# q and k written as high and low parts, and the output norm's root in fused VectorE steps

## The chip, the cores and the metric

One Trainium2 chip, of which the program uses one core. The metric is the device time of one execution of the program in microseconds (us): the median of several runs. One further execution was taken with the hardware profiler; the rows below are from that one.

The core has a matrix engine (PE in the rows; PEld is its weight load, which overlaps), VectorE (DVE), ScalarE (ACT), GpSimd (POOL) and SyncE (SP). SP does no arithmetic here: it issues the DMAs, in the order of its queue. All five run their own instruction lists in order and wait for each other through semaphores. PE writes to PSUM; the other data lie in SBUF, and larger arrays in DRAM.

## The reference

A decoder layer on 1024 rows of 1024 columns: a norm, one wide input projection, three branches (a convolution, a differential attention with 8 heads, a cross-attention into 256 memory rows), and an output projection. The change touches the attention branch:

```
q = rms_norm(q.reshape(B, S, H, 2, d), qn_g)          # H = 8 heads, 2 maps of d = 64
k = rms_norm(k.reshape(B, S, H, 2, d), kn_g)
s = q k^T * scale + bias;  s = where(dist >= 0, s, -inf);  p = softmax(s)
a = p[:, :, 0] - lam * p[:, :, 1]                     # one map minus lam times the other
o = a v
o = rms_norm(o, subln_g) * (1 - lambda_init) * silu(gate)
```

All is fp32. PE multiplies fp32 data that are rounded to a shorter form (fp32r), so the kernel splits an operand x into a high part H = round(x) and a low part L = x - H and adds the products H·H, H·L and L·H.

## The kernel before, in words

The program has stages that follow each other on PE: norms and memory projections; a convolution input and cross-attention; a stage in which the wide projection is computed by blocks of seven products instead of eight (`Quads`, `strassen`; PE lines L640); attention, into whose gaps the projections of the other branches are filled (PE lines L79 to L81 of `mm3`); and a tail with the rest of those, the last branch projection and the output projection.

**PE's order is fixed at build time** (`manual_schedule` for PE). In attention a planner in the program writes it: it keeps due times for every step (`t_of`), books estimated work on DVE, ACT and POOL (`run`), and takes, at each point, the step that is ready first; where nothing would be ready for more than 0.4 us it puts in a piece of six filling matmuls. The filling work is a list of 40 banks; what is not used in attention runs behind it. The other engines' orders and that of SP's queue are made by a scheduler from priorities.

**q and k.** `qk_out` ends a 128x512 tile of q or k (head h, i = 0 for q and 1 for k, half j): square, split, two matmuls with a matrix of means, logarithm and exponential for the root, and two DVE steps; the finished tile goes to DRAM by one DMA (`qT`, `kT`, L777). There are 32 such tiles. In attention `project(h)` loads a half of a head (`load`): q twice, into partitions 0 to 63 and 64 to 127 (`qf`), k likewise (`kf`), and v (`vf`): five DMAs. `cut` then makes the operands: ACT rounds all of q and of k (L962), and POOL subtracts, four instructions for a half (L968), so that the operand `q` holds the high part above its low part, `k` the high part twice and `kL` the low part twice. `turn` transposes v on PE (L973). `qf`, `kf` and `vf` have one buffer each.

**Scores.** A group is a head and 256 of its rows (32 groups). `pair` does for 128 rows of a group four matmuls (L1001, L1003) per 512 columns and a DVE step per map that adds the distances and takes the maximum (L1007, `mx`); behind the last columns follow small DVE steps (L1018, L1019 `nm`), the exponentials on ACT (L1021), and DVE steps that form p0 + c·p1 (L1025). POOL copies the reciprocal of the first sum to `r0` (L1027).

**Values and the output norm.** `trans` and `prod` transpose p and multiply it with v (L1045, L1053). Behind the last product of a group ACT copies the sum to `o` (L1058), and `norm` follows: two squares with row sums on ACT (L1067), the helper `rstd_of` with the root (a logarithm and an exponential on ACT, L175 and L176, and one Newton step in five POOL instructions, L174 and L177 to L180), one more POOL product (L1070), and two DVE products (L1072). `turned` then transposes `o` on PE (L1079) and gates it.

Of the kernel before, what the change touches and what calls it, by code (L numbers as in the profile page):

```python
# [30 lines left out]
def hybrid_layer(  # L31
# [361 lines left out]
    qT, kT, oT = [[tc.dram_tile([P, S], F32, name=f"{n}{h}") for h in range(DH)] for n in ("qT", "kT", "oT")]  # L393
# [165 lines left out]
    with ExitStack() as st:  # L559
# [186 lines left out]
        def qk_out(h):  # L746

            def f(i, j, ps):
# [11 lines left out]
                def means():  # L760
# [16 lines left out]
                    nc.sync.dma_start((qT, kT)[i][h][:, j * 512:j * 512 + 512], ps)  # L777
# [157 lines left out]
    with ExitStack() as st:  # L935
# [9 lines left out]
        def project(h):  # L945
# [4 lines left out]
            def load(half):  # L950
                sl = slice(half * 512, half * 512 + 512)
                T["f", half] = [new(ap_, [P, 2, 512], n, bufs=1) for n in ("qf", "kf")]
                for f, src in zip(T["f", half], (qT, kT)):
                    for r in (slice(0, 64), slice(64, P)):
                        nc.sync.dma_start(f[r], src[h][:, sl].rearrange("(m p) s -> p m s", m=2))
                T["vf", half] = vf = new(ap_, [P, 512], "vf", bufs=1)
                T["loaded", half] = nc.sync.dma_start(vf, vT[h // 2][h % 2 * P:h % 2 * P + P, sl])

            def cut(half, x):
                f = T["f", half][x]  # L960
                high = T["qk"[x], half] = new(ap_, [P, 2, 512], "qk"[x], F32R, bufs=3)
                nc.scalar.copy(high, f)  # L962
                low = high
                if x:
                    low = T["kL", half] = new(ap_, [P, 2, 512], "kL", F32R, bufs=3)
                r = slice(0 if x else 64, P)
                for m in range(2):
                    nc.gpsimd.tensor_tensor(low[r, m, :], f[r, m, :], r2f(high[r, m, :]), op=ALU.subtract)  # L968
# [7 lines left out]
            return T, load, cut, turn  # L976

        def scores(h, g, T, A):
# [4 lines left out]
            for t in range(2):  # L983
# [4 lines left out]
                for hf in range(nh):  # L988
                    def pair(t=t, i=i, n=n, hf=hf, nh=nh, R=R):
                        if t == 0 and hf == 0:  # L990
                            A["r0"] = new(tiny, [P, 2], "r0", bufs=4)
# [23 lines left out]
                        rc = new(tiny, [P, 2], "rc")  # L1015
# [11 lines left out]
                        nc.gpsimd.tensor_copy(A["r0"][:, t:t + 1], rc[:, 0:1])  # L1027
# [35 lines left out]
        def norm(A):  # L1063
            o, ss, y = A["o"], new(tiny, [P, 2], "oss"), new(tiny, [P, 2], "osy")
            junk = new(ap_, [P, P], "ojunk", bufs=1)
            for t in range(2):
                nc.scalar.activation(junk, o[:, t * P:(t + 1) * P], AF.Square, scale=A["r0"][:, t:t + 1],  # L1067
# [338 lines left out]
```

## Time and profile before

| what | value |
|---|---|
| median of 3 runs | 1758.54 us (1756.33 to 1763.14) |
| profiled execution, its own time | 1758.3 us |
| its span (first to last instruction) | 1756.5 us |
| mean granted PE clock | 0.979 |
| PE busy | 1655.1 us (94%) |
| DVE, ACT, POOL busy | 1289.3, 920.1, 862.1 us |

The busy share of an engine is a mean over stages with different limits. What counts for a change is the stage in which it lies, and what PE waits for there. The clock column says what share of full speed (2.4 GHz) PE's clock had; it is either full or half.

### The profile page before, as it was taken

What the parts mean: (1) busy time and instruction counts of PE and PEld (TensorE: products, weight loads), DVE (VectorE), ACT (ScalarE), POOL (GpSimd) and SP (SyncE); (2) the same over time, 40 slices, a digit from 0 to 9 for tenths busy, and PEclk for the clock granted to TensorE, in tenths of its full rate; (3) what the DMA queues carried; (4) which work ended last, traced back from release to release, by engine and by line L of the source; (5) the groups of instructions that cost most, each with busy time, mean ns of one, the idle gap of its engine ahead of it and who ended that gap; (6) DMA issues with size and microseconds to landing.
All of it is one profiled execution on the core that took longest, in us unless ns stands there. A gap on an engine that the chain in (4) does not pass through costs nothing. (4 is left out here: it accounts for less than half of the span.)

```text
span 1756.5 us, 24408 instructions
## 1 busy us (share of the span) xinstructions
PE 1655.1 (94%) x7882; PEld 1371.2 (78%) x7882; DVE 1289.3 (73%) x2196; ACT 920.1 (52%) x1949; POOL 862.1 (49%) x895
## 2 busy tenths in 40 slices
PE   6999999999999997898789999999897999999999
PEld 5788888878888885777678888877786878877787
DVE  7869997999999997987664856734666676676911
ACT  5614645344444453575556865753766776763300
POOL 3220111687555554445555666544557564557820
PEclk8999999999999998899899999999999999999999
DMA  7410212332323436845663323288478455465632
GB/s 267 141 39 25 75 63 76 108 108 91 122 77 113 133 108 191 262 161 182 226 220 99 108 90 109 96 293 250 149 234 263 125 174 157 152 226 202 196 118 90
DMA packets 208313, 260.11 MB, mean 148 GB/s; under 512 B 16145, under 2 KB 110358, under 8 KB 208184
## 3 DMA queue, kind: packets, MB, share of 16 engines
q1 hardware_dynamic: 208184, 258.55, 45.7%
q8 instruction: 62, 1.02, 0.2%
q14 instruction: 67, 0.55, 0.1%
HBM read 180.89 MB, written 77.59 MB: 147 GB/s over the span
## 5 line engine op out<-in xcount | busy, mean ns | idle before, releaser
L423 DVE SCALAR_TENSOR_TENSOR cv<-u,cw,cv 128x512 f32<-128x512 f32 x464 | 349.2, 753 | 10.4
L114 POOL TENSOR_TENSOR wL<-wraw,wH 128x512 fp32r<-128x512 f32 x104 | 143.7, 1397 | 254.3 <-ACT wH L113 156.9
L79 PE MATMUL mm<-hH,wH 128*128 128x512 f32 x512 | 205.8, 402 | 0.6 <-DVE sg L1147 0.6
L81 PE MATMUL mm<-hH,wL 128*128 128x512 f32 x512 | 200.8, 392 | 0.0
L80 PE MATMUL mm<-hL,wH 128*128 128x512 f32 x512 | 200.7, 392 | 0.0
L623 POOL TENSOR_TENSOR wL<-ws,wH 128x512 fp32r<-128x512 f32 x76 | 103.9, 1367 | 187.6 <-ACT wH L622 183.1
L622 ACT CAST wH<-ws 128x512 fp32r<-128x512 f32 x152 | 93.3, 619 | 155.7 <-PE tp L640 126.1
L640 PE MATMUL tp<-hH,wH 128*128 128x512 f32 x304 | 124.8, 411 | 27.4 <-ACT sx L645 27.4
L1007 DVE CUSTOM_DVE_ANT_0 p<-sc,dist 128x512 f32<-128x512 f32 (+3 forms) x192 | 100.4, 551 | 57.4 <-PE sc L1003 57.1
L640 PE MATMUL tp<-hL,wH 128*128 128x512 f32 x304 | 123.7, 407 | 0.0
L1021 ACT ACTIVATE p<-p,nm 128x768 f32<-128x768 f32 (+7 forms) x128 | 98.3, 770 | 48.4 <-DVE nm L1019 48.2
L640 PE MATMUL tp<-hH,wL 128*128 128x512 f32 x304 | 123.3, 406 | 0.0
L623 POOL TENSOR_TENSOR wL<-wraw,wH 128x512 fp32r<-128x512 f32 x76 | 110.1, 1449 | 17.9 <-ACT wH L622 17.5
L618 POOL TENSOR_TENSOR ws<-wraw,wraw 128x512 f32<-128x512 f32 x76 | 111.4, 1465 | 6.8 <-DVE T3L L85 0.6
L622 ACT CAST wH<-wraw 128x512 fp32r<-128x512 f32 x114 | 70.5, 619 | 81.9 <-PE sc L640 29.6
L81 PEld LDWEIGHTS mm<-hH,wL 128*128 128x128 f32 x512 | 96.6, 189 | 21.0
L79 PEld LDWEIGHTS mm<-hH,wH 128*128 128x128 f32 x512 | 96.9, 189 | 18.1 <-DVE sg L1147 0.8
L80 PEld LDWEIGHTS mm<-hL,wH 128*128 128x128 f32 x512 | 97.0, 189 | 17.5
L113 ACT CAST wH<-wraw 128x512 fp32r<-128x512 f32 (+1 forms) x112 | 64.4, 588 | 66.9 <-PE mm L81 34.7
L640 PEld LDWEIGHTS tp<-hH,wH 128*128 128x128 f32 x304 | 60.2, 198 | 43.8 <-ACT sx L645 31.2
L618 POOL TENSOR_TENSOR ws<-ws,wraw 128x512 f32<-128x512 f32 x38 | 57.3, 1507 | 70.3 <-issue 28.0
L645 ACT COPY sx<-tp 128x512 f32<-128x512 f32 x152 | 88.2, 580 | 0.4 <-DMA gxTH<-sx 0.4
(303 smaller groups left out, 4750.2 us busy)
## 6 DMA issues: line engine op xcount, KB each, us to landing
wraw<-in_w_in_dram SPq DMA_DIRECT2D x184, 256.0 KB, 3.1
sg<-sgT SPq DMA_DIRECT2D x65, 256.0 KB, 3.4
sgT<-sx SPq DMA_DIRECT2D x48, 256.0 KB, 2.2
qf<-qT SPq DMA_DIRECT2D x32, 256.0 KB, 4.7
kf<-kT SPq DMA_DIRECT2D x32, 256.0 KB, 4.4
yT<-sg SPq DMA_DIRECT2D x32, 256.0 KB, 2.6
acc<-cvT SPq DMA_DIRECT2D x30, 256.0 KB, 3.5
mw<-in_w_mem_kv_dram SPq DMA_DIRECT2D x16, 256.0 KB, 7.1
```

Source lines behind the costliest of these rows:

```text
L79: nc.tensor.matmul(ps, lhsT=lh, rhs=rh, start=start, stop=False)
L80: nc.tensor.matmul(ps, lhsT=lh, rhs=rl, start=False, stop=False)
L81: nc.tensor.matmul(ps, lhsT=ll, rhs=rh, start=False, stop=stop)
L114: self.low(kk).tensor_tensor(L[:, :w], raw[:, :w], r2f(H[:, :w]), op=ALU.subtract)
L423: nc.vector.scalar_tensor_tensor(ps if j < CONV_K - 1 else acc, u[:, at - j:at - j + 512], cw[:, c, 30 - j:31 - j], ps, op0=ALU.mult, op1= ...
L618: nc.gpsimd.tensor_tensor(o, a, b, op=op)
L622: nc.scalar.copy(H, a)
L623: (nc.gpsimd if n in (1, 3, 4, 6) else nc.vector).tensor_tensor(L, a, r2f(H), op=ALU.subtract)
L640: nc.tensor.matmul(R[bank], lhsT=l[:, ks], rhs=r, start=start and k == 0 and i == 0, stop=stop and k == 3 and i == 2, skip_group_check=True)
L645: last[0] = nc.scalar.copy(R[n], R[bank])
L1007: nc.vector.tensor_tensor_reduce(out=pm[m][:, k0:k0 + w], in0=sc[m][:, :w], in1=dist[:, d0:d0 + w], scale=1.0, scalar=-3.0e38, op0=ALU.add ...
L1021: nc.scalar.activation(pm[m][:, :n], pm[m][:, :n], AF.Exp, bias=nm[:, m:m + 1], scale=slope, accum_out=sm[:, m:m + 1])
```

## The change

Three things are changed, and the planner's figures with them.

- `qk_out` splits the finished tile at once (an ACT cast to H, a DVE subtraction to L) and stores both, in `qkT`. `load` brings the parts straight into the operands: `q` from high and low, `k` twice from the high part, `kL` twice from the low part, v as before: seven DMAs for a half, with three buffers for the operands and two for `vf`. `cut` is gone.
- `norm` no longer calls `rstd_of`: the Newton step is one ACT square and three DVE instructions, the product with `r0` is joined to the last DVE step, and POOL's copies to `r0` are gone.
- The planner waits for `load` instead of `cut`, lets v's transposes run in a stream of their own (`turn`), books the norm as ACT and DVE work with 1.0 us behind it instead of a chain of 8.0 us, and takes a load as 8.0 us instead of 3.0.

```
-    qT, kT, oT = [[tc.dram_tile([P, S], F32, ...) ...
+    qkT = [[[tc.dram_tile([P, S], F32, name=f"{n}{x}{h}") for x in "HL"] for n in "qk"] for h in range(DH)]
...
-                    nc.sync.dma_start((qT, kT)[i][h][:, j * 512:j * 512 + 512], ps)
+                    H, L = root.bitcast(F32R), ps.bitcast(F32R)
+                    split(H, L, ps)
+                    for dst, x in zip(qkT[h][i], (H, L)):
+                        nc.sync.dma_start(dst[:, j * 512:j * 512 + 512], r2f(x))
...
-                T["f", half] = [new(ap_, [P, 2, 512], n, bufs=1) for n in ("qf", "kf")]
-                for f, src in zip(T["f", half], (qT, kT)):
-                    for r in (slice(0, 64), slice(64, P)):
-                        nc.sync.dma_start(f[r], src[h][:, sl].rearrange("(m p) s -> p m s", m=2))
-                T["vf", half] = vf = new(ap_, [P, 512], "vf", bufs=1)
+                (qh, ql), (kh, kl) = qkT[h]
+                for n, parts in (("q", (qh, ql)), ("k", (kh, kh)), ("kL", (kl, kl))):
+                    t = T[n, half] = new(ap_, [P, 2, 512], n, F32R, bufs=3)
+                    for p0, src in zip((0, 64), parts):
+                        nc.sync.dma_start(r2f(t[p0:p0 + 64]), src[:, sl].rearrange("(m p) s -> p m s", m=2))
+                T["vf", half] = vf = new(ap_, [P, 512], "vf", bufs=2)
...
-            def cut(half, x):
-                f = T["f", half][x]
-                high = T["qk"[x], half] = new(ap_, [P, 2, 512], "qk"[x], F32R, bufs=3)
-                nc.scalar.copy(high, f)
...
-                    nc.gpsimd.tensor_tensor(low[r, m, :], f[r, m, :], r2f(high[r, m, :]), op=ALU.subtract)
...
-                        nc.gpsimd.tensor_copy(A["r0"][:, t:t + 1], rc[:, 0:1])
+                        A["r0"].append(rc[:, 0:1])
...
-            rstd_of(y, ss, [P, 2], 1.0 / P, 1e-6, eps6, pool=tiny, tags=("onv", "ont"))
-            nc.gpsimd.tensor_tensor(y, y, A["r0"], op=ALU.mult)
+            nc.vector.tensor_scalar(v, ss, 1.0 / P, 1e-6, op0=ALU.mult, op1=ALU.add)
+            nc.scalar.activation(x, ss, AF.Ln, bias=eps6[:, 0:1], scale=1.0 / P)
+            nc.scalar.activation(y, x, AF.Exp, scale=-0.5)
+            nc.scalar.activation(x, y, AF.Square)
+            nc.vector.scalar_tensor_tensor(x, x, -0.5, v, op0=ALU.mult, op1=ALU.mult)
+            nc.vector.scalar_tensor_tensor(y, x, 1.5, y, op0=ALU.add, op1=ALU.mult)
             for t in range(2):
-                nc.vector.tensor_scalar_mul(o[:, t * P:(t + 1) * P], o[:, t * P:(t + 1) * P], y[:, t:t + 1])
+                sl = slice(t * P, t * P + P)
+                nc.vector.tensor_scalar(o[:, sl], o[:, sl], y[:, t:t + 1], A["r0"][t], op0=ALU.mult, op1=ALU.mult)
...
-        PARTS, SLACK, HOP, CHAIN, LOAD, AB, CHUNK, FIRST = 4, 1.25, 0.3, 8.0, 3.0, 3, 3.0, 11.0
+        PARTS, SLACK, HOP, LOAD, AB, CHUNK, FIRST = 4, 1.25, 0.3, 8.0, 3, 3.0, 11.0
...
-                    t_of["o", n] = run("DVE", run("ACT", t_of["av", n], 0.17, 0.17) + CHAIN, 0.17, 0.17)
+                    x = run("ACT", t_of["av", n], 0.36, 0.36, 0.2, 0.2, 0.2)
+                    t_of["o", n] = run("DVE", x, 0.08, 0.08, 0.2, 0.2) + 1.0
...
-        streams = {k: [] for k in ("load", "prod", "trans", "pair", "norm2")}
+        streams = {k: [] for k in ("load", "turn", "prod", "trans", "pair", "norm2")}
```

PE's instructions are the same in number and kind, and their order is the same up to the beginning of attention. From there it differs. On PE, before, the second transposes of head 0's v (`vf`) stood 54 filling matmuls behind the first, and 36 more behind the second came the first scores (`sc`). The rows at the second transposes of before:

```order
L79 MATMUL mm<-hH_100,wH 128x512
L80 MATMUL mm<-hL_102,wH 128x512
L81 MATMUL mm<-hH_100,wL 128x512
L79 MATMUL mm<-hH_101,wH 128x512
L80 MATMUL mm<-hL_103,wH 128x512
L81 MATMUL mm<-hH_101,wL 128x512
```

and those at the only transposes of head 0 in the changed kernel, which stand where the first ones of before stood, behind the first 54 filling matmuls:

```order
L81 MATMUL mm<-hH_101,wL 128x512
L967 MATMUL tp<-ident,vf 128x128 x8
L995 MATMUL sc<-k,q 128x512
L997 MATMUL sc<-kL,q 128x512
L995 MATMUL sc<-k,q 128x512
L997 MATMUL sc<-kL,q 128x512
L79 MATMUL mm<-hH_101,wH 128x512
L80 MATMUL mm<-hL_103,wH 128x512
L81 MATMUL mm<-hH_101,wL 128x512
```

Both halves of v are now transposed together and the first scores stand directly behind them: 90 filling matmuls that were ahead of the scores have moved behind them.

On SP's queue, at the loads of head 0 (`sg` is a gate of a filling bank, `yT` the store of a finished one, `hH` and `hL` an operand of the filling work), before:

```order
L1102 DMA sg<-sgT 128x512
L955 DMA qf<-qT_1089 64x2x512 x2
L955 DMA kf<-kT_1097 64x2x512 x2
L1119 DMA yT_89<-sg 128x512
L957 DMA vf<-vT_1113 128x512
L1102 DMA sg<-sgT 128x512 x2
L893 DMA hH_100<-gxTH 128x4x512
L893 DMA hL_102<-gxTL 128x4x512
```

and now:

```order
L781 DMA kH_1127<-w_10878 128x512
L781 DMA kL_1128<-sx 128x512
L1101 DMA sg<-sgT 128x512
L960 DMA q<-qH_1097 64x2x512
L960 DMA q<-qL_1098 64x2x512
L960 DMA k<-kH_1099 64x2x512 x2
L1118 DMA yT_89<-sg 128x512
L960 DMA kL<-kL_1100 64x2x512 x2
L962 DMA vf<-vT_1129 128x512
L960 DMA q<-qH_1097 64x2x512
L960 DMA q<-qL_1098 64x2x512
L960 DMA k<-kH_1099 64x2x512 x2
```

The 14 loads of head 0 stand in a row, behind the stores of the last k tile's two parts and around one `yT`; the loads of `hH` and `hL` have moved behind them and behind seven more loads of head 1.

On DVE, around the norm of a group in the changed kernel (`onv`, `ont`, `osy` and `o` are its tiles):

```order
L1001 ISA mx 128x1
L1063 TENSOR_SCALAR onv<-oss 128x2
L1117 TENSOR_TENSOR sg<-mm,sg 128x512
L1013 TENSOR_SCALAR nm<-mx 128x2
L1067 SCALAR_TENSOR_TENSOR ont<-ont,onv 128x2
L1068 SCALAR_TENSOR_TENSOR osy<-ont,osy 128x2
L1071 TENSOR_SCALAR o<-o,osy,rc 128x128 x2
```

where POOL had, before:

```order
L174 TENSOR_SCALAR onv<-oss 128x2
L1027 COPY r_11550<-rc 128x1
L177 TENSOR_TENSOR ont<-osy 128x2
L178 TENSOR_TENSOR ont<-ont,onv 128x2
L179 TENSOR_SCALAR ont<-ont 128x2
L180 TENSOR_TENSOR osy<-osy,ont 128x2
L1070 TENSOR_TENSOR osy<-osy,r_11362 128x2
```

Six POOL steps have become three small DVE steps and one on ACT, and they stand in DVE's queue between scores and filling work.

## Rows read from the trace of the kernel before

**Rows 1.** The page, part 1: busy us of each engine.

```profile
PE 1655.1 (94%) x7882; PEld 1371.2 (78%) x7882; DVE 1289.3 (73%) x2196; ACT 920.1 (52%) x1949; POOL 862.1 (49%) x895
```

**Rows 2.** Stretches: length, PE, PEld, DVE, ACT, POOL busy us (instructions), clock, DMA share, GB/s.

```profile
960.00:1000.00 40.00, 40.00 (x175) 32.39 (x174) 33.76 (x39) 34.03 (x63) 25.53 (x19) 1.00 0.32 100
...
1160.00:1200.00 40.00, 38.36 (x170) 30.85 (x169) 12.50 (x15) 16.07 (x26) 17.14 (x14) 1.00 0.98 327
...
1600.00:1640.00 40.00, 38.73 (x171) 31.52 (x170) 31.17 (x32) 13.77 (x24) 34.60 (x24) 1.00 0.79 269
```

**Rows 3.** PE's waits, 1176 to 1680 us: total us, times, longest.

```profile
PE sc L1001 <- DVE mx L1007: 11.9, 10, 3.4
PE tp L1079 <- DVE o L1072: 10.4, 2, 7.6
```

**Rows 4.** Timeline of PE: two of those waits, in brackets.

```profile
1233.32 0.51 PE L1001 MATMUL sc<-k,q 128*128 128x512 f32 x1 [3.43 <-DVE mx L1007]
...
1347.75 0.66 PE L1079 MATMUL tp<-ident,o 128*128 128x128 f32 x2 [7.57 <-DVE o L1072]
```

**Rows 5.** Busy times by stretches, behind the longest wait; columns as in rows 2.

```profile
1348.00:1352.00 4.00, 4.00 (x18) 3.31 (x18) 0.69 (x1) 1.26 (x3) 1.47 (x2) 0.60 1.06 389
```

**Rows 6.** Timeline of POOL ahead of the end of that wait.

```profile
1332.66 2.56 POOL L968 TENSOR_TENSOR kL<-kf,k 128x512 fp32r<-128x512 f32 x2
1335.30 3.50 POOL L968 TENSOR_TENSOR q<-qf,q 64x512 fp32r<-64x512 f32 x2
...
1347.08 0.20 POOL L1070 TENSOR_TENSOR osy<-osy,r 128x2 f32<-128x2 f32 x1
```

**Rows 7.** Timeline of ACT and DVE: the norm of one undisturbed group.

```profile
1358.35 0.37 ACT L1058 COPY o<-av 128x256 f32<-128x256 f32 x1 [1.01 <-PE av L1053]
...
1362.00 0.19 ACT L176 ACTIVATE osy<-ont 128x2 f32<-128x2 f32 x1
...
1364.31 0.48 DVE L1072 TENSOR_SCALAR o<-o,osy 128x128 f32<-128x128 f32 x2
```

**Rows 8.** Timeline of SP's queue at head 0's first half.

```profile
1178.64 0.49 SPq L1102 DMA_DIRECT2D sg<-sgT  x1
1179.18 1.31 SPq L955 DMA_DIRECT2D qf<-qT  x2
...
1183.75 0.33 SPq L1119 DMA_DIRECT2D yT<-sg  x1
1184.12 0.43 SPq L957 DMA_DIRECT2D vf<-vT  x1
...
1189.87 0.58 SPq L955 DMA_DIRECT2D qf<-qT  x1
```

**Rows 9.** Timeline of PE: the transposes of head 0's v.

```profile
1188.55 0.66 PE L973 MATMUL tp<-ident,vf 128*128 128x128 f32 x4
...
1202.58 0.66 PE L973 MATMUL tp<-ident,vf 128*128 128x128 f32 x4 [1.11 <-DMA vf<-vT]
```

**Rows 10.** Timeline of ACT and DVE between the stages.

```profile
1177.36 1.28 ACT L943 ACT_TABLE_LOAD   x1
...
1183.03 0.69 DVE L1118 TENSOR_TENSOR sg<-mm,sg 128x512 f32<-128x512 f32 x1 [6.28 <-DMA sg<-sgT]
...
1202.01 1.05 ACT L962 CAST q<-qf 128x1024 fp32r<-128x1024 f32 x1 [12.13 <-DMA qf<-qT]
```

**Rows 11.** The instructions of line L1019: ns least, median, most.

```profile
L1019 DVE TENSOR_SCALAR nm<-mx x64: 152/170/1301, 1215.3 to 1580.9; 128x2 f32<-128x2 f32 x64
```

**Rows 12.** Groups, 940 to 1176 us: busy us, mean ns | idle before.

```profile
L85 DVE TENSOR_TENSOR ms<-w,ms 128x512 fp32r<-128x512 f32 x32 | 35.2, 1099 | 21.2 <-ACT ms L84 21.2
```

**Rows 13.** Groups of instructions on POOL from 1205 to 1602 us.

```profile
L114 POOL TENSOR_TENSOR wL<-wraw,wH 128x512 fp32r<-128x512 f32 x32 | 42.4, 1343 | 5.7 <-ACT wH L113 5.1
L968 POOL TENSOR_TENSOR q<-qf,q 64x512 fp32r<-64x512 f32 x29 | 39.0, 1365 | 6.6 <-ACT q L962 5.6
L968 POOL TENSOR_TENSOR kL<-kf,k 128x512 fp32r<-128x512 f32 x30 | 38.2, 1292 | 16.4 <-ACT k L962 11.7 <-DMA yT<-sg 4.7
```

More of the change, by code (lines that the diff above doesn't have):

```diff
@@ L1208, in pair_step @@
             w, last_ = min(512, P * (i + 1) - hf * 512), (i + 1) * P <= hf * 512 + 512
-            needs = [("cut", h, i // 4), ("cut", h, hf)] + ([("turned", n - 4)] if hf == 0 and n >= 4 else [])
+            needs = [("load", h, i // 4), ("load", h, hf)] + ([("turned", n - 4)] if hf == 0 and n >= 4 else [])
             def after(at):
@@ L1254, in turned_step, with load_steps @@
             return f, [("o", n)], lambda: tps[0], 0.214, after
-        def load_steps(h, half, load, cut, turn):
+        def load_steps(h, half, load, turn):
             old = h - 1 - half
             gone, read = [[(e, old, g) for g in range(0 if half else 2, 4)] if old >= 0 else [] for e in ("done", "read")]
-            prev_ = [("turn", h, 1)] if not half else [("turn", h - 1, 0)] if h else []
+            turns = [("turn", h - 1, half)] if h else []
             def loaded(at):
                 t_of["load", h, half] = at + {(0, 1): FIRST, (0, 0): FIRST, (1, 1): 2 * FIRST}.get((h, half), LOAD)
-            def cut_(at):
-                x = run("ACT", max(at, t_of["load", h, half]), 0.95)
-                y = run("POOL", x, 1.2, 1.2)
-                t_of["cut", h, half] = run("POOL", max(y, run("ACT", x, 0.95)), 1.2, 1.2)
             def turned(at):
@@ L1274, in turned @@
                 tps.append(tps.pop(0))
-            return [(lambda: load(half), prev_, lambda: -1.0, 0, loaded),
-                    (lambda: (cut(half, 0), cut(half, 1)), read + [("load", h, half)], lambda: -1.0, -1, cut_),
+            return [(lambda: load(half), read + turns, lambda: -1.0, 0, loaded),
                     (lambda: turn(half), gone + [("load", h, half)], lambda: tps[0], 4 * 0.107, turned)]
-        streams = {k: [] for k in ("load", "prod", "trans", "pair", "norm2")}
+        streams = {k: [] for k in ("load", "turn", "prod", "trans", "pair", "norm2")}
         c = 0
@@ L1283, in hybrid_layer @@
                 for half in (1, 0):
-                    streams["load"] += load_steps(h, half, *heads[h][1:])
+                    for k, step in zip(("load", "turn"), load_steps(h, half, *heads[h][1:])):
+                        streams[k].append(step)
             trans, prod = values(h, g, T, A)
```

17 lines of the change are left out of this document (6 added, 11 removed).

## The prediction

> **What bounds the kernel now.** The busy times come first: PE is busy for 1655 of 1756.5 us, no other engine for more than 1289 [rows 1]. So the end is set by PE's work, which the change leaves as it is, and by the times in which PE waits. I look for those by stretches: in the seven-product stage PE has none (960 to 1000 us: 40.00 of 40), though DVE has 33.76 and ACT 34.03 [rows 2]. At the step into attention the DMA engines are the full ones: 0.98 of their time and 327 GB/s from 1160 to 1200 [rows 2]. Then the list of PE's waits says what there is to win from 1176 us on: 11.9 us for the maximum of scores on DVE, in ten waits, and 10.4 us for the normed `o`, in two, one of them 7.6 [rows 3]. The timeline of PE puts these in place: 3.43 us at 1233 in front of a score, 7.57 us at 1348 in front of a transposition of `o` [rows 4]. Behind the long one PE's clock was at its lower level for a while: 0.60 granted on average from 1348 to 1352 [rows 5], so 0.4 of 4 us is lost there, 1.6 us more. All of this is about 24 us of 1758, and the change has to find its gain there, since whatever it takes from ACT and POOL is not waited for as such.
>
> Why `o` came late at 1348 can be read on POOL: the last step of its norm ran at 1347.08, and ahead of it the queue had the subtractions for `kL` and `q`, 2.56 and 3.50 us, among others [rows 6]. In an undisturbed group the same chain, from ACT's copy at 1358.35 to the second product's end at 1364.79, took 6.4 us, of which 2.1 lie between the exponential's end (1362.19) and the start of DVE's products (1364.31), POOL's part [rows 7].
>
> The base of the sum is the profiled execution, 1758.3 us (its span and 1.8 outside); the median of the runs, 1758.5, is the same within what counts here.
>
> **Seven-product stage (A).** It gains 32 ACT casts, 32 DVE subtractions and 32 more stores. The nearest row for the subtraction is the same helper's on another tile there: 1.10 us [rows 12], so 35 us on DVE in all; ACT's casts are shorter. PE's work does not wait for the stored parts, so the price is nothing as long as DVE keeps up. A q/k job has 92 matmuls; at the 0.23 us that 54 of them take between the transposes at 1188.55 and 1202.58, less the wait [rows 9], that is 21 us with four tiles, so 40 us get 7.6 tiles and 8.4 us of DVE. From 960 to 1000 this makes 33.8 + 8.4 = 42 of 40: overfull, and what is late next is the mean-square split that PE's means matmul needs. I take 2 us of waits, with bounds of 0 (the next stretch has room) and 8 (such a surplus in each of the stretches with two q/k jobs in a row). One more ACT cast among the last copies that PE waits for adds about 0.7. A = +2.7.
>
> **Loads of head 0 (B).** PE still reaches head 0's transposes behind 54 filling matmuls, at 1188.5 plus the 0.7 of A, but now all 14 loads must have landed by then, where it was five [rows 8, 9]. They also start later. The last k tile's cast stands behind ACT's table load, which ended at 1178.64 [rows 10]; with a cast, a subtraction (1.10 at most) and two stores ahead of it on SP, `sg` goes out about 1180.5 and not at 1178.64 [rows 8]. Four loads of 0.65 us each (1.31 for two) bring the queue to 1183.5. Then stands `yT`, which waits for DVE's product, which waits for `sg`: that landed at 1183.03 [rows 10], 4.4 us behind its issue, and `yT` went at 1183.75; shifted with `sg`, about 1185.7. Ten loads behind it take 6 us, so the last is issued at 1192, and from `vf`'s issue at 1184.12 to its transposition it took 4.4: 1196. PE waits for 7 us, as long as the wait of rows 4, with the same 1.6 us at the low clock; the 1.1 us at 1202 [rows 9] goes. B = +7.5. From below: if `yT` holds nothing up, the last is issued at 1190 and lands at 1193 to 1194: +4 and no loss of clock. From above: the second half's loads of before, issued from 1189.87, were all there for ACT at 1202.01 [rows 8, 10], 12 us; as long behind 1189 would be +13. The bytes agree: 14 x 262 kB at 327 GB/s [rows 2] are 11.2 us.
>
> **First scores (C).** From the first scores on, DVE is the slow one: it needs a maximum, two small steps and a combination for each 128 rows, and PE waited 3.43 us at 1233 [rows 4]; I count 5.0 us of the 11.9 here, with a shorter wait right behind, and 1.6 at the low clock as after the other long wait [rows 5]. The small step `nm` takes 170 ns in the median but 1301 at most [rows 11]; the long ones lie where POOL runs large subtractions. Of those large POOL instructions the change removes 77 us (`q`, `kL`) and leaves the 42 of `wL` [rows 13]. So I take half of 6.6 us: C = -3, bounds 0 and -6.6. Here a rule of the Trainium skill bears: "Advanced Engine Details and Errata", section VectorE Performance Modes, says that VectorE's second SBUF port is shared with GpSimd, so that GpSimd's instructions and VectorE's two-port ones block each other. Rows 11 agree in that the same 2-column step takes up to eight times as long. The rule also speaks against the other half of the change: the new DVE steps can then be blocked by a `wL` of 1.3 us each, and by it D would be some 10 us worse, by the median row it would not.
>
> **Output norm (D).** The 10.4 us and the 1.6 at the low clock go: -12. In their place the planner, which now books a shorter chain, puts the transposes of `o` nearer. Counting PE's order between a group's last product and its transposes, with 0.23 us for 512 columns and half of that for the short ones, they stood 10 to 24 us behind; now 4.3 to 15, ten of the 32 at 7 us or less. The chain of rows 7 loses POOL's 2.1 us and gets one ACT square (0.19 as the exponential) and two DVE steps of 0.17 in the median [rows 11] or a little more, so 5.0 to 5.5 us if nothing is in its way. Then two groups fall short, by 1.9 us in all. Queues of ACT and DVE make a chain longer by one to three us (one combination or two exponentials ahead of it) in a third of the groups; for the ten near ones I take 4 us more. D = -12 + 6 = -6, bounds -11 and +1 (chain of 7.5 us throughout: 13 us of waits).
>
> **The rest.** E: the other score waits of rows 3 (11.9 - 5.0 = 6.9 us): ACT loses 32 casts of 1.05 us [rows 10], DVE gets 96 small steps but fewer blockings: -2, bounds -5 and +3. F, the tail: by the order 174 filling matmuls stand behind the last transposes, where it was 60, so that the loads of the last branch are covered, but the loads of partial sums and weights that lay under attention come closer together, where DMA had 0.79 already [rows 2]: +1, bounds -2 and +8. More bytes in the seven-product stage and in attention (8.4 MB each) lie where DMA has 0.3 of its time [rows 2]: 0. The freed ACT and POOL times have no price of their own, since PE did not wait for them elsewhere.
>
> Sum: 2.7 + 7.5 - 3 - 6 - 2 + 1 = +0.2, so 1758.5; I say 1759 us. A gain in attention's waits is paid back at attention's start.
>
> **Rivals.** *Faster, 1741 us:* the waits behind POOL are the main thing. If the first scores no longer wait (-6.6), the norm falls short nowhere but in two groups (-10), the other score waits halve (-4) and the loads are at their lower bound (+4) with A at 0.7 and F at -1.3: -17. For it: both long waits for `o`, and the long `nm`, lie under POOL's queue [rows 6, 11]. Against it: the 14 loads. The same rule on the shared port would make it so, as a mechanism of this kernel: 77 us less of blocking POOL work [rows 13]. *Slower, 1775 us, the short transposes:* the new chain sits in the queues of ACT and DVE, which are fuller than POOL. At 7.5 us for every group the ten near ones cost 13 us; at 8.5 us, some 23. It decides from about 8 us on: -12 + 23 = +11, with A and B +21, less C and E +16. For it: DVE and ACT are in order and busy for most of attention. Against it: 6.4 us with POOL's 2.1 in it [rows 7]. *Slower, 1772 us, the start:* loads at their upper bound (+13) and DVE overfull in the seven-product stage (+8), with C to F as above (-10) and 0.7: +12. *No effect of the norm:* if the two waits had another cause than POOL, D is +6 and the time 1770; rows 6 speak against it.
>
> **Chances.** The forecast, within 0.5% (8.8 us, about what a measurement of this kernel can tell from no change) 0.40; faster by more 0.32; short transposes 0.13, the start and the rest 0.15, so slower by more 0.28. The range is from 1742 to 1776, from the faster rival's time to the slower one's; the forecast's own is 1751 to 1767.
>
> **What would show it.** In the new profile: a wait of PE of 4 to 9 us at head 0's transposes (L967), with SP's `yT` standing in the middle of the loads (B right); no wait of PE from 960 to 1160 beyond 2 us (A); waits for `o` spread over several groups of 0.5 to 2 us instead of two long ones (D), L1013 near 0.17 us in the mean (C). Wrong: no wait at the transposes, or waits for `o` that sum to more than 10 us, or new waits for `sg` or weights in the tail.

## The result: 1.7% slower, and the profile after

The changed kernel takes 1788.89 us in the median of 4 runs (1785.30 to 1792.74), the kernel before 1760.38 in the same comparison: a ratio of 1.0173, with an interval of 1.0153 to 1.0193. The prediction was 1759 us with a range up to 1776: it was wrong, by 30 us. The profiled execution took 1791.09 us with a span of 1789.3.

The page's busy times of the changed kernel, against [rows 1]:

```profile
PE 1665.7 (93%) x7882; PEld 1378.0 (77%) x7882; DVE 1311.9 (73%) x2324; ACT 910.2 (51%) x1981; POOL 723.3 (40%) x575
```

POOL has 139 us less to do, ACT 10 less, DVE 23 more, and PE has the same 7882 matmuls. Nothing in this line says that the kernel is slower. The stretches of [rows 2] do, with one more, 1200 to 1240:

```profile
960.00:1000.00 40.00, 37.04 (x160) 29.34 (x158) 35.07 (x41) 32.35 (x60) 23.36 (x16) 1.00 0.36 120
1160.00:1200.00 40.00, 37.59 (x157) 30.17 (x156) 20.11 (x24) 23.27 (x41) 17.92 (x14) 0.96 0.92 327
1200.00:1240.00 40.00, 29.13 (x136) 24.09 (x134) 16.21 (x52) 9.45 (x19) 0.00 (x0) 0.83 0.93 265
1600.00:1640.00 40.00, 35.69 (x150) 28.60 (x149) 20.08 (x25) 8.99 (x17) 23.98 (x19) 0.96 0.88 313
```

From 960 to 1000 PE now has 3 us of waits where it had none, and 160 matmuls where it had 175. From 1200 to 1240 it is idle for 11 us and its clock is 0.83 on average, at the lower level for a third of the time. PE's waits, first of the seven-product stage (940 to 1205 us), then of attention (1190 to 1610 us), against [rows 3]:

```profile
PE av L765 <- DVE ms L85: 5.1, 4, 1.4
PE mm L765 <- DVE ms L85: 3.0, 4, 0.8
PE tp L641 <- ACT sx L646: 2.4, 2, 1.9
PE av L765 <- ACT ms L84: 1.2, 1, 1.2
...
PE tp L1078 <- DVE o L1071: 13.9, 7, 4.9
PE tp L967 <- DMA vf<-vT: 10.9, 2, 5.9
PE sc L995 <- DVE mx L1001: 5.6, 6, 3.0
PE av L1047 <- ACT a L1041: 3.5, 2, 3.4
PE av L1047 <- ACT o L1052: 3.0, 1, 3.0
PE tp L1078 <- ACT osy L1065: 1.3, 1, 1.3
```

The two long waits for `o` have become seven, and their sum has grown from 10.4 to 13.9 us; the means matmuls wait for 9.3 us (the three rows of L765), head 0's transposes for 10.9. In the kernel before, the means matmuls (L764 there) waited from 940 to 1205 us only here:

```profile
PE mm L764 <- DVE ms L85: 0.8, 1, 0.8
```

A list of waits leaves out what the lower clock costs, and two traces whose PE orders differ can't be laid over each other by time. So I matched them by PE's work: every matmul counts 0.2268 us for 512 columns, shorter ones in proportion, and a 128-column transposition 0.11 us. What a stretch takes beyond the sum of its matmuls is its *loss*. Short products with v take longer than so counted, some 40 us in all, in every kernel alike, so only differences mean something. The stretches are those of equal work, named by their times in the kernel before. The last two columns are experiments below.

| stretch | before | changed | e10 (looser plan) | e15 (from before) |
|---|---|---|---|---|
| 960 to 1160, seven-product stage | 1.8 | 13.3 | 12.7 | 1.8 |
| 1160 to 1205, start of attention | 3.7 | 19.3 | 18.9 | 6.7 |
| 1205 to 1259, first scores | 11.4 | 8.0 | 8.6 | 8.5 |
| 1259 to 1600, attention | 64.3 | 72.9 | 53.8 | 54.8 |
| 1600 to the end | 7.1 | 7.2 | 5.4 | 8.9 |

The changed kernel loses 32.4 us more than the one before, and its span is 32.8 longer: 11.5 in the seven-product stage, 15.6 at the start of attention, -3.4 at the first scores, 8.6 in attention, nothing in the tail.

**At the start of attention** the timeline of SP's queue and of PE:

```profile
1195.43 0.43 SPq L1101 DMA_DIRECT2D sg<-sgT  x1
1195.91 0.68 SPq L960 DMA_DIRECT2D q<-qH  x1
...
1199.00 0.34 SPq L1118 DMA_DIRECT2D yT<-sg  x1
...
1206.65 0.33 SPq L962 DMA_DIRECT2D vf<-vT  x1
...
1207.83 1.12 PE L967 MATMUL tp<-ident,vf 128*128 128x128 f32 x4 [5.01 <-DMA vf<-vT]
1214.80 1.11 PE L967 MATMUL tp<-ident,vf 128*128 128x128 f32 x4 [5.85 <-DMA vf<-vT]
```

From `sg`'s issue to that of the last `vf` it takes 11.2 us (the prediction had 11.5), but its transposition starts 8.2 us behind that issue, where I had taken 4.4.

**In the seven-product stage** the timeline of DVE and PE at one of the waits:

```profile
975.28 1.76 DVE L85 TENSOR_TENSOR ms<-w,ms 128x512 fp32r<-128x512 f32 x1
976.97 1.77 DVE L85 TENSOR_TENSOR sx<-sx,w 128x512 fp32r<-128x512 f32 x1
...
977.10 0.51 PE L765 MATMUL av<-ms,maps 128*128 128x512 f32 x1 [1.45 <-DVE ms L85]
```

PE waits for the low part of the mean squares, which DVE finishes at 977.04. The new subtraction (`sx`) follows it here and delays the next steps; elsewhere it stands ahead. It takes 873 ns in the mean, and the mean-square split 1199 where it took 1099 [rows 12].

The first row shows a second thing: the awaited split took 1.76 us itself. Of the 32 splits the eleven that ran beside no POOL instruction took 0.68 to 0.69 us, in both kernels. Those of more than 1.5 us all ran beside a POOL instruction on two tensors; before there were 8 of them, now there are 15, and seven of the eight splits in the first two rows of L765 above are such. The later steps of DVE thus fall beside POOL's more often.

### The profile page after: what moved, and what is told of

The parts are those of the page before. It is cut to its first block, busy times and chain, and to the rows that moved or that the text cites. A ratio compares the mean times of both kernels' runs of the same rounds, so it can differ in the third digit from the quotient of the medians.

```text
span 1789.3 us, 24241 instructions
## 1 busy us (share of the span) xinstructions
PE 1665.7 (93%) x7882; PEld 1378.0 (77%) x7882; DVE 1311.9 (73%) x2324; ACT 910.2 (51%) x1981; POOL 723.3 (40%) x575
## 4 chain that ended last, share of the span: by engine, by line
PE 61%; DVE 15%; DMA 12%; issue 5%; ACT 5%; POOL 2%; SPq 0%; DVEq 0%; ACTq 0%; POOLq 0%
PE tp L641 17%; PE mm L79 7%; PE mm L81 7%; PE mm L80 7%; PE sc L641 7%; PE mm L641 4%; PE av L1047 3%; DMA acc<-cvT 2%; PE sc L995 2%; PE sc L997 1%; DVE p L1001 1%; DVE cv L424 1%; DVE sg L1356 1%; PE tp L1039 1%; DMA gcH<-w 1%
## 5 line engine op out<-in xcount | busy, mean ns | idle before, releaser
L424 DVE SCALAR_TENSOR_TENSOR cv<-u,cw,cv 128x512 f32<-128x512 f32 x464 | 349.2, 753 | 10.4
L624 POOL TENSOR_TENSOR wL<-ws,wH 128x512 fp32r<-128x512 f32 x76 | 110.8, 1457 | 194.8 <-ACT wH L623 190.6
L1082 POOL TENSOR_TENSOR oT<-oT,gd 128x256 f32<-128x256 f32 x32 | 25.6, 803 | 256.4 <-ACT oT L1081 185.1
L624 POOL TENSOR_TENSOR wL<-wraw,wH 128x512 fp32r<-128x512 f32 x76 | 110.5, 1453 | 16.2 <-ACT wH L623 16.0
L81 PEld LDWEIGHTS mm<-hH,wL 128*128 128x128 f32 x512 | 97.5, 190 | 21.5
L79 PEld LDWEIGHTS mm<-hH,wH 128*128 128x128 f32 x512 | 98.3, 192 | 18.2 <-DVE sg L1146 0.9
```

The source lines that it names most:

```text
L79: nc.tensor.matmul(ps, lhsT=lh, rhs=rh, start=start, stop=False)
L81: nc.tensor.matmul(ps, lhsT=ll, rhs=rh, start=False, stop=stop)
L424: nc.vector.scalar_tensor_tensor(ps if j < CONV_K - 1 else acc, u[:, at - j:at - j + 512], cw[:, c, 30 - j:31 - j], ps, op0=ALU.mult, op1= ...
L624: (nc.gpsimd if n in (1, 3, 4, 6) else nc.vector).tensor_tensor(L, a, r2f(H), op=ALU.subtract)
```

## Experiments

The table has the ratio to the kernel before, run on the same chip, with its interval, and the loss of three stretches in the run's one profile. The nine kernels that have the changed kernel's own order on PE from attention on lose 69 to 79 us in attention; a difference of less than about 5 us there, from one profile, says little. The profiled execution can lie off the median: by 9 us below it in e4 and in e5 (means later), by 11 above it in e7.

| kernel | median us | ratio (interval) | seven-product | start | attention |
|---|---|---|---|---|---|
| e1, norm alone | 1774.5 | 1.0091 (1.0076 to 1.0106) | 1.9 | 3.9 | 71.8 |
| e2, parts alone | 1787.9 | 1.0176 (1.0157 to 1.0196) | 12.6 | 16.9 | 72.9 |
| e3, margin | 1786.5 | 1.0162 (1.0143 to 1.0180) | 12.7 | 18.3 | 74.2 |
| e4, loads booked longer | 1797.4 | 1.0220 (1.0197 to 1.0242) | 12.8 | 21.5 | 72.8 |
| e5, means later | 1812.9 | 1.0301 (1.0275 to 1.0326) | 37.1 | 16.9 | 74.1 |
| e5, split later | 1785.3 | 1.0144 (1.0124 to 1.0165) | 12.4 | 16.3 | 70.8 |
| e6, split on POOL | 1789.1 | 1.0168 (1.0144 to 1.0192) | 18.2 | 17.1 | 75.0 |
| e7, wide loads | 1800.2 | 1.0235 (1.0213 to 1.0258) | 35.1 | 18.5 | 69.3 |
| e9, no subtraction | 1779.9 | 1.0114 (1.0082 to 1.0146) | 7.1 | 15.2 | 78.8 |
| e9, stores alone | 1773.0 | 1.0084 (1.0056 to 1.0113) | 1.9 | 18.5 | 71.7 |
| e8, chain 9 (before) | 1762.6 | 1.0023 (1.0007 to 1.0038) | 1.8 | 4.3 | 64.0 |
| e8, chain 7 (before) | 1759.1 | 0.9994 (0.9972 to 1.0017) | 1.9 | 4.1 | 67.2 |
| e10, looser plan | 1769.0 | 1.0051 (1.0036 to 1.0066) | 12.7 | 18.9 | 53.8 |
| e11, weights earlier | 1788.0 | 1.0164 (1.0142 to 1.0185) | 13.3 | 16.7 | 69.7 |
| e12, weights on DVE | 1782.8 | 1.0129 (1.0112 to 1.0146) | 12.7 | 16.6 | 75.2 |
| e13, three edits | 1763.1 | 1.0026 (1.0011 to 1.0041) | 12.7 | 15.7 | 54.1 |
| e14, weights on DVE (before) | 1760.1 | 1.0016 (1.0003 to 1.0029) | 1.8 | 5.0 | 64.0 |
| e15, all weights on DVE (before) | 1748.7 | 0.9937 (0.9917 to 0.9958) | 1.8 | 6.7 | 54.8 |

**Each half alone, and the planner's numbers.** e1 is the kernel before with the new norm and its place in the planner, e2 the changed one with the old norm; e3 and e4 change one number each of the changed kernel's planner:

```
e3:  t_of["o", n] = run("DVE", x, 0.08, 0.08, 0.2, 0.2) + 5.0        (was + 1.0)
e4:  FIRST = 24.0                                                    (was 11.0)
```

> The kernel before with the new norm alone (DVE and ACT steps, the product with r0 joined, and the planner's new cost for it); q and k are stored, loaded and cut as before. Theory 'distance': the new chain of the norm is no shorter in practice than the old one (7.6 us in the median in both traces), since its steps queue on ACT and DVE, while PE's order has the transposes of o 3.5 us nearer on average (10.7 us behind the last product where it was 14.2). Then PE waits for o in four or more groups, 6 to 12 us in all, and the time is 1757 to 1766 us against 1760 of the kernel before. Rival 'loads': attention lost its time to the fourteen loads and what queues behind them on SP; the norm by itself frees POOL and helps. Then the waits for o fall below 4 us and the time is 1747 to 1754 us.

> The changed kernel with the old norm (root on POOL, copies to r0, a chain of 8.0 us in the planner); q and k as high and low parts stay. Theory 'distance': with the transposes of o 13.2 us behind the last products again and POOL free of the large subtractions, the waits for o fall from 13.9 us to 4 or less; time 1776 to 1782 us where the changed kernel has 1789. Rival 'loads': the time stays at 1785 to 1791 us, and the waits for o, for a and for scores stay in the sum.

> The changed kernel with one number of the planner changed: 5.0 us instead of 1.0 behind the norm's booked steps, so that the transposes of o stand 12.5 us behind the last product on average, where it was 9.5. Theory 'distance': waits for o fall from 13.9 us to 4 or less, time 1777 to 1782 us. Rival 'loads' (late because ACT and DVE wait for data of late loads): the waits stay, 1785 to 1791 us.

> The changed kernel with one number of the planner changed: the loads of head 0 are taken as 24 us instead of 11, so that 114 filling matmuls stand ahead of head 0's transposes where it was 54 (13.6 us more). Theory: the 10.9 us of waits at these transposes, and some 2 to 3 us of PE at its lower clock around them, go: 1775 to 1780 us. Rival: the wait only moves, since the filling work drawn ahead is missing in later gaps and the loads behind are as late: 1784 to 1790 us.

The norm alone costs 16 us, and its 1774.5 us lie above the range of 'distance'. PE waits for `o` in eight places, as 'distance' says, but for 13.9 us in all instead of 6 to 12; the waits in attention up to 1590 us and behind it:

```profile
PE tp L1084 <- DVE o L1077: 11.8, 5, 4.4
PE sc L1001 <- DVE mx L1007: 10.8, 13, 3.4
...
PE mm L80 <- DVE GL L85: 5.6, 3, 2.4
```

But only some 7 us of the 16 are lost in attention; the tail loses 9 us more than before (16.2 where it was 7.1), since only 42 filling matmuls are left behind the last transposes, where the kernel before had 60, and DVE's split of the last heads' `o` (`GL`) is late for them. e8 with chain 9, below, also leaves 42 and has the same waits.

e2 and e3 go against 'distance': with the transposes of `o` 13.2 and 12.5 us behind the last products again, both times are within 3 us of the changed kernel's. In e3 the waits for `o` are gone, and others stand in their place (attention, 1215 to 1615 us):

```profile
PE sc L995 <- DVE mx L1001: 12.2, 12, 4.3
PE av L1047 <- ACT a L1041: 7.6, 6, 2.1
PE tp L1039 <- ACT oT L1081: 2.2, 1, 2.2
```

'Loads' does not stand either, since e1 has none of the new loads and loses as much in attention. In e4 the wait at head 0's transposes goes, and PE waits for 10.3 us on `sg` instead, whose load stands behind the fourteen:

```profile
PE mm L79 <- DVE sg L1117: 10.3, 1, 10.3
```

The wait moved, as the rival said. The median is 8.5 us above the changed kernel's, more than the rival said, but the six times fall apart into two near 1789 us, the profiled one among them, and four from 1797 to 1803; what the four lose more isn't known.

**What the seven-product stage pays for.** Five edits of `qk_out` in the changed kernel: the means matmuls later, the subtraction on POOL, the split one step later, then parts of it left out.

```
e5 means later:  due.append([AFTER + 1, means])                      (was AFTER; and bufs=6 for `ms`)
e6:              nc.gpsimd.tensor_tensor(L, ps, r2f(H), op=ALU.subtract)
e5 split later:  due.append([1, parts])        # parts: the split and its stores
e9 no subtraction: nc.scalar.copy(H, ps)       # no subtraction, L is ps itself
e9 stores alone: H, L = ps.bitcast(F32R), ps.bitcast(F32R)
```

> The changed kernel with the means matmuls of q and k one step of the seven-product stage later in PE's order (12 matmuls or more, about 3 us; one more buffer for their operands). Theory 'late link': PE lost 11.5 us between 960 and 1172 us because a tile's new subtraction stands ahead of the next tile's mean-square subtraction on DVE, and the means matmul comes too early for that; with 3 us more room nearly all of it goes: time 1776 to 1781 us where the changed kernel has 1789, PE's waits on L765 below 2 us. Rival 'full': DVE has no room for 32 more subtractions, and PE waits for it wherever the matmul stands: 1786 to 1791 us.

> The changed kernel with the 32 subtractions for the stored low parts on POOL instead of DVE. Theory 'late link': DVE's queue is as before and the waits on L765 fall from 9 us to 2 or less, if POOL's longer instructions do not slow DVE's by as much: 1777 to 1783 us. Rival 'full', or DVE's steps held up as much by POOL's as by its own: 1786 to 1792 us.

> The changed kernel with the split of the stored tile put one step later in the program; on DVE this moves 8 of the 32 subtractions behind the mean-square subtraction of the next tile, and nothing else. Theory 'late link': these eight are the ones that PE waited for, 3 to 9 us of 11.5 go: 1780 to 1786 us. Rival 'full': no change, 1787 to 1791 us.

> The changed kernel with the 32 subtractions for the stored low parts left out of the seven-product stage (the tile itself is stored as its low part, so the scores are of other numbers); the casts, the 64 stores and all loads stay. Theory 'subtraction': the 32 DVE instructions, 0.9 us each in the mean, are what makes the mean-square subtractions late; the loss between 960 and 1172 us falls from 13 us to 4 or less, time 1776 to 1781 us. Rival 'tiles': the tile is held longer until its store, or the cast on ACT counts as much, and the loss stays at 8 us or more: 1783 to 1790 us.

> The changed kernel with neither the cast nor the subtraction in the seven-product stage: the finished tile is stored twice (so the scores are of other numbers); the 64 stores and all loads stay. Theory 'compute': the loss between 960 and 1172 us is as in the kernel before, 2 us; time 1774 to 1779 us. Rival 'stores': the second store, by SP's queue or by holding the tile, costs by itself; the loss stays above 6 us and the time above 1781 us.

With the stores alone the loss is that of the kernel before, 1.9 us; with the cast as well 7.1, with the subtraction too 13.3. So the cast costs about 5 us and the subtraction about 6, and the 32 stores nothing. The number of mean-square splits of more than 1.5 us goes with it: 8 with the stores alone, as before, 12 with the cast, 15 with the subtraction too. The edits that were to mend it failed. The means later: PE's waits on L765 are gone, but the tiles are held longer, and the copies into the next ones wait for a free one (940 to 1205 us):

```profile
PE tp L641 <- ACT sx L646: 29.1, 6, 7.7
```

On POOL the subtraction is worse (18.2, with 18 long splits). The later split moved eight subtractions and the stage's loss stayed at 12.4: the place of these eight is not the cause, and its 3 us less in the whole are within the uncertainty of the two ratios. Neither 'late link' nor 'full' says it well. DVE is not full (35.07 of 40 us, above). My reading, which no run tests by itself, is that DVE and ACT hand a tile to each other several times, in queues that hold the next tile's steps as well, that both the cast and the subtraction make these links later, and that more of DVE's steps then run beside POOL's. How the cost divides between the place in the queue and POOL is open: no run takes POOL's work out of this stage.

**The rate of the loads.** e7 lays the parts side by side in DRAM, so that one DMA fills 128 partitions:

```
-  nc.sync.dma_start(r2f(t[p0:p0 + 64]), src[:, sl].rearrange("(m p) s -> p m s", m=2))     # twice
+  nc.sync.dma_start(r2f(t), src[:, sl].rearrange("(m p) s -> p m s", m=2))
```

> The changed kernel with q's two parts, k's high part twice and k's low part twice laid side by side in DRAM, so that each operand of a half comes by one DMA into 128 partitions instead of two into 64 each: the same bytes, four loads for a half instead of seven; in exchange 192 stores of half a tile each in the seven-product stage where there were 64 of a whole one (k's parts are stored twice). Theory 'narrow': the loads into 64 partitions are what moves slowly (233 to 275 GB/s at full DMA engines, where 128-partition loads had 390), so the 14 loads' 19 us become 12 to 14 and the wait at head 0's transposes falls from 10.9 to 6 us or less: 1778 to 1784 us. Rival 'bytes': the rate is the same whatever the shape, the wait stays: 1787 to 1793 us.

The whole is worse, because three times as many stores cost the seven-product stage 22 us. The rate, though, is what 'narrow' said. One stretch among the loads of the changed kernel, then one of e7 (columns as in [rows 2]):

```profile
1200.00:1215.00 15.00, 4.13 (x18) 2.92 (x17) 0.00 (x0) 0.58 (x1) 0.00 (x0) 0.71 1.05 259
```

```profile
1232.00:1237.00 5.00, 1.11 (x4) 0.71 (x4) 0.00 (x0) 0.58 (x1) 0.00 (x0) 0.62 1.05 397
```

The DMA engines are full in both; where nearly all loads go to 64 partitions they get 259 GB/s, where all go to 128 partitions 397. The Trainium skill, "DMA: Bandwidth & Descriptors", section Rules for kernel authors, advises one 128-partition transfer instead of two to disjoint halves, and this agrees. (e7 also gives k's second copies a place of their own in DRAM; that isn't separated from the shape.) Of the wait nothing was won. The waits of e7 around head 0's transposes (1205 to 1245 us):

```profile
PE tp L968 <- DMA vf<-vT: 8.9, 2, 4.7
PE mm L79 <- DVE sg L1118: 3.1, 1, 3.1
```

At the transposes PE waits for 2 us less than in the changed kernel, but for 3.1 us on `sg` just ahead of them. From the first load of `q` to the last transposition of v it takes 15.5 us (18.9 in the changed kernel), not the 12 to 14 of 'narrow': in SP's queue eight half-tile stores stand ahead of the eight loads and `yT` in their middle, and the rate was 297 GB/s from 1225 to 1230 us and 326 from 1230 to 1235.

**Is the order of before a lucky one?** The kernel before with the norm's chain taken as 9.0 and 7.0 us instead of 8.0 (`CHAIN`).

> The kernel before with one number of its planner changed: 9.0 us for the norm's chain instead of 8.0; no instruction is added or removed. Theory 'fitted order': the 7 to 9 us that attention loses behind its first groups in every changed version so far, whichever part is undone, are the price of any other order on PE than the one of before, which suits the waits of its neighbours by choice; then this kernel is slower by 4 to 14 us: 1762 to 1772 us. Rival 'mechanism': the loss comes from the new norm and the new loads themselves, and this kernel stays within 4 us of the kernel before: 1754 to 1762 us.

> The kernel before with 7.0 us for the norm's chain in the planner instead of 8.0. Theory 'fitted order': slower by 4 to 14 us, 1762 to 1772 us, though the waits for o change little. Rival 'mechanism': within 4 us of the kernel before, or, by the shorter distances alone, at most 5 us of more waits for o.

'Fitted order' falls: attention loses 64.0 and 67.2 us in these, 64.3 before. What the changed versions lose there is theirs.

**Why attention loses.** e10 gives the changed kernel's planner more room, e11 asks for weights earlier, e12 takes their subtractions off POOL.

```
e10:  SLACK = 1.35  (was 1.25),   ... + 5.0  (was + 1.0)
e11:  (3, Wp["x"][1]), (11, Wp["c"][0]), (19, Wp["c"][1]), (27, Wd[0][0]), (31, Wd[0][1])   (were 5, 13, 21, 29, 33)
e12:  Wd = [[cols(w_diff_proj[0], i * 512, lambda kk: nc.vector, ks=ks) ...                 (was nc.gpsimd)
```

> The changed kernel with two numbers of its planner changed: all booked work on DVE and ACT 1.35 times the estimate instead of 1.25, and 5.0 us behind the norm instead of 1.0. PE's order then has 876 filling matmuls ahead of the last transposes of o (786 in the changed kernel, 900 before), which stand 12.9 us behind the last products on average (9.5; 14.2 before). Theory 'tight plan': attention behind its first groups lost 8.6 us more than before because the planner, with the loads, the cuts and the long chain no longer booked, moved 26 us of filling work behind attention and lets PE run into late ACT and DVE steps; with the work back, 5 to 8 us go: 1780 to 1784 us where the changed kernel has 1789. Rival 'late data' or 'ports': the waits are of a kind that room does not cure; they move to other instructions, 1786 to 1792 us.

> The changed kernel with the weights of the filling work asked for two banks (about 10 us) earlier in the program; PE's order is the same. Theory 'late data': ACT's casts wait 12 us for weights in attention, and the copies that PE needs (a, o) stand behind them in ACT's queue; the 3.4 and 3.0 us at 1385 and 1394 us and what follows go: 1781 to 1785 us. Rivals 'tight plan' and 'ports': 1786 to 1791 us.

> The changed kernel with the subtractions for the filling work's weights on DVE instead of POOL (0.69 us each there, 1.3 us on POOL); PE's order is the same. Theory 'ports': the norm's small DVE steps are long only while POOL subtracts (0.16 us without, up to 1.24 us with it), and that makes the chain late; without it the waits for o fall from 14 us to 7 or less, and 4 to 7 us go: 1782 to 1786 us. Rivals: the steps are late by their place in the queues, and 22 us more of work on DVE make it no better: 1787 to 1796 us.

The looser plan brings 20 us, more than 'tight plan' said: attention's loss falls from 72.9 to 53.8 us, ten less than in the kernel before. Its instructions are those of the changed kernel; only their order differs, PE's and with it that of the others. So attention's loss came from the order that the planner had made. Its waits, 1215 to 1615 us:

```profile
PE sc L995 <- DVE mx L1001: 8.3, 7, 2.4
PE av L1047 <- ACT a L1041: 3.8, 3, 1.6
...
PE tp L1078 <- DVE o L1071: 0.7, 1, 0.7
```

Two things change together in it. In the changed kernel 786 filling matmuls stand ahead of the last transposes, and these are 9.5 us behind their products; e3 restores the distance (12.5) with 744, e2 too (13.2) with 774, e1 has 918 with 10.7: all lose 72 to 74 us in attention. e10 has 876 with 12.9 and loses 53.8. That both are needed fits these kernels and isn't shown: `SLACK` gives room to all other booked steps of DVE and ACT as well, and no run changes it alone.

Earlier weights change nothing: 'late data' falls. e12, as it ran, moved only the last branch's 16 subtractions (the trace has POOL at 37 others; its edit for the other branches had no effect); waits for `o` fell to 9.6 us, attention's loss did not, and its 6 us less lie in the tail, where the wait of 3.3 us for `YH` was missing. In e13 that wait is there again, 3.1 us, so that gain isn't one to count on.

**Together, and without the change.** e13 is e10, e12 and the later split in one; e14 and e15 give the kernel before the weights' subtractions on DVE, e14 those of the last branch and e15 all that attention uses, with PE's order as it was:

```
e15:  Wp = {n: [cols(..., lambda kk, n=n: nc.gpsimd if n == "o" else nc.vector, ks=ks) ...     and Wd as in e12
```

> The changed kernel with three edits at once: the looser planner (1769 us by itself), the weights' subtractions on DVE (6 us, nearly all of them in the tail, where a wait of 3.3 us for the last branch's operand and the lower clock behind it went), and the later split of the stored tile (3 us by itself, within its uncertainty). Theory: the two sure ones add up, since one acts in attention and one in the tail: 1760 to 1765 us, no faster than the kernel before, because the seven-product stage's 12 us and the loads' 15 us stay. Rival: the weights' subtractions on DVE take back what the looser order gave in attention: 1768 to 1775 us.

> The kernel before with the filling weights' subtractions on DVE instead of POOL, nothing of the change. Theory 'POOL': the two long waits for o of the kernel before (10.4 us) came from POOL's full queue, and the tail's wait of 3.0 us from POOL's blocking of DVE; with 55 us off POOL most of both goes: 1745 to 1755 us, faster than both kernels. Rival: 27 us more on DVE in attention make the waits for scores longer by as much: 1757 to 1765 us.

> The kernel before with all of attention's weight subtractions on DVE. The two kernels e12 and e14 moved only the last branch's 16 subtractions, and the trace of e14 has POOL at the same weights ahead of the late o, which waited 7.0 us; here the other branches' go too, about 45 us off POOL. Theory 'POOL': the waits for o (10.4 us before) fall to 4 or less and the time is 1747 to 1755 us. Rival: the large subtractions for kL and q on POOL, or DVE's longer queue, hold up as much: 1756 to 1766 us.

e13 comes to 1763 us, as expected: no faster than the kernel before, with the seven-product stage and the start unmended. e14 does not help: POOL still has the other branches' weights ahead of the late `o`. e15 is the fastest kernel here, 0.6% under the kernel before. Its first waits, 1215 to 1615 us:

```profile
PE sc L1001 <- DVE mx L1007: 7.6, 7, 2.6
PE mm L80 <- DVE GL L85: 2.5, 1, 2.5
```

No wait for `o` is left, and attention loses 54.8 us instead of 64.3 with the same order on PE. So the reading of [rows 6], that POOL's queue made `o` late, is shown, though the subtractions for `kL` and `q`, which the prediction named, stayed on POOL; and the gain which the change was to bring there is had by moving POOL's other work.

## Why the prediction was wrong, by its steps

**A, seven-product stage: right in what comes late, wrong in why and in size.** I took 2.7 us with a bound of 8.7; 11.5 were lost by 1160, mostly at the mean-square split that I had named. The step that failed is "the price is nothing as long as DVE keeps up": I priced the subtraction by DVE's sum, 42 of 40 us, and the cast at 0.7. DVE kept up, with 35 us of 40, and PE waited all the same; the cast alone costs 5 us, the subtraction 6 (e9). POOL, beside which 15 instead of 8 splits became long, wasn't in the term at all.

**B, loads of head 0: right in kind, off in size.** Forecast 7.5, bound 13, measured 15.6. The queue went as worked out, to 0.3 us. The term that was too small is the landing, 4.4 us from a row of a single load of v, where it measured 8.2: twelve of the fourteen loads go to 64 partitions, and the full DMA engines move 259 GB/s; I had checked the bytes against 327, the mean of a stretch with other loads in it. The rest is the clock, 0.83 granted from 1200 to 1240: I had 1.6 us of loss, and beyond the waits themselves some 5 us more than before are lost from 1160 on.

**C, first scores: right.** -3 forecast, -3.4 measured; no wait at the first scores is left. L1013 (`nm`) ran beside a POOL subtraction or product in 10 of 64 cases, before in 35. e15, with PE's order of before and less on POOL, loses 8.5 us there, about as little as the changed kernel.

**D and E, the norm and the other waits: wrong in sign.** Forecast -8, measured +8.6. The cause read from the trace was right (e15), and the gain is there: e10 gets 10.5 us less loss in attention than the kernel before. What failed is "D = -12 + 6": I counted the nearer transposes one by one against a chain of 5 to 5.5 us. The chain, from the end of the last product to the end of the second DVE product, was 7.6 us in the median, as long as before, though POOL's part was gone; that its steps now queue on ACT and DVE is the rival *short transposes*, named at 0.13, and its 13 us of waits at 7.5 us per chain are close to the 13.9 measured. By the prediction's own bound that makes D +1, not what was measured. And the distances weren't the whole: e3 lengthened them and won nothing. The planner had also taken 114 filling matmuls, 26 us of work that waits for no step of attention, out of attention. I saw that number and used it only in F, as cover for the tail. In attention it is cover too; that late steps of ACT and DVE stopped PE because this cover was gone fits e10, which has 90 of the 114 back, but no run puts back the filling work alone.

**F, the tail: right**, +1 forecast, 0.1 measured.

So the two slower rivals, the start and the short transposes, came true together, at 1772 and 1775 by themselves, and the range held each but not both. (The start's own terms, 13 + 8 - 10 + 0.7, give 1770.) The start also went beyond its bounds: A and B took 27.1 us where that rival had 21.7. The rule on the shared port, from the Trainium skill ("Advanced Engine Details and Errata", section VectorE Performance Modes), agrees with what was measured step by step, below; what it would add to D, 10 us, isn't separately shown, since no run took POOL's subtractions wholly away from beside the new norm.

What stays open: how the looser plan's gain divides between the distances, the filling work and the rest that `SLACK` moves, and how the seven-product stage's cost divides between the queues and POOL.

## What to carry to other kernels

Work that leaves an engine with room (POOL and ACT in attention) for a stage in which two engines pass a tile to and fro is paid there, even if neither is full: 32 casts and 32 subtractions cost 11.5 us of PE's time here. Price such work by what comes late behind it, not by busy time. Where a program plans its own order, a cheaper step makes the plan tighter too; count the independent work that the new order takes out of a stage, and give the plan its room back before judging the change. And bytes are to be divided by the rate of loads of the same shape, not by the mean of a stretch.

## What the runs showed of the hardware

- A DVE step on 2 columns took 0.15 to 0.17 us whenever no POOL product or subtraction of two tensors ran beside it, without an exception in 122 such steps of the changed kernel (`onv`, `ont`, `osy`, `nm`). Beside one, 38 steps took 0.42 to 0.97 us in the mean by kind, up to 1.24. Two of the lines (ns least, median, most):

```profile
L1068 DVE SCALAR_TENSOR_TENSOR osy<-ont,osy x32: 146/161/1237, 1244.6 to 1602.3; 128x2 f32<-128x2 f32 x32
L1013 DVE TENSOR_SCALAR nm<-mx x64: 147/170/1224, 1221.1 to 1584.4; 128x2 f32<-128x2 f32 x64
```

- The same holds for a large step: DVE's subtraction of 128x512 for the mean squares took 0.68 to 0.69 us beside no POOL instruction and up to 1.79 beside POOL instructions on two tensors.
- With the DMA engines full, loads that went nearly all into 64 partitions moved at 259 GB/s, loads into 128 partitions at 397.
- Short waits cost PE more than their length: in the stretch of attention in the table PE was idle for 27.4 us in the changed kernel and 21.8 in the one before, and its clock was at the lower level for 13.6 us, in four places, where it had been for 6.8, in one.
